# Another written order for the up-projection's prologue and units in a one-core hybrid decoder layer

## The chip, the cores and the metric

One core of a Trainium2 chip. The core has TensorE (PE, matrix products into PSUM banks), VectorE (DVE), ScalarE (ACT) and GpSimd (POOL), and SyncE (SP), which here only issues transfers. Each engine runs its own instructions in the order in which the program gives them, and waits on semaphores for the others. Transfers are issued from SP's, ACT's and POOL's queues. The metric is the device time of one execution in microseconds; given are the median, the lowest and the highest of three runs.

## The reference, cut to what matters

The kernel computes one decoder layer on 512 tokens of 1024 channels: a modulated norm, an input projection, two groups of attention-like heads, an output projection, then a gated MLP. The change is in the first half of the MLP:

```python
h2 = rmsnorm(x, norm2_g[l]) * (1.0 + sc2) + sh2
u = causal_dwconv(h2 @ w_up[l], conv_w[l], conv_b[l])      # w_up: 1024 x 5632
a, v = jnp.split(u, 2, axis=-1)
x = x + gt2 * ((jax.nn.silu(a) * v) @ w_down[l])           # w_down: 2816 x 1024
```

All arrays are f32, and the products are made to f32 accuracy.

## The kernel before

**Products.** Every f32 operand is split into a high and a low part (hi is the operand rounded to the PE's f32 form by a cast on ACT, L149; lo is the operand minus hi, a subtraction on DVE, L150), and a product is three matmuls: hi x hi, hi x lo, lo x hi (`mm3`, L152 to L155). The up-projection goes column by column: 22 pairs of a gate column block and a value column block, each 128 wide, so 44 *steps* numbered st. A step multiplies 8 blocks of weights with all 512 tokens: 24 matmuls of 128x512, into one PSUM bank `u`. After a step comes `up_post(st)`: bias and last tap of the convolution on ACT (L1621), the two other taps on DVE (L1622, L1623), silu on ACT (L1626) for a gate step, and for a value step the gate product (L1629) and then a list of small *work items* that split the result for the down-projection (L1801 and L150 on DVE, L149 on ACT; two parts are parked in memory by ACT's queue, L1831 and L1832).

**Units.** Steps 8 to 23 are done in four *units* j = 2 to 5 of four steps. In a unit the first two steps (4j, 4j+1) are not made as 48 full matmuls but, in the manner of Strassen and Winograd, as seven products of half size (P1 to P7, each 12 matmuls of 128x256) on sums and differences of weights and of tokens. The other two steps (4j+2 and 4j+3, called B and C) are standard and are cut into B0, B1 and C0, C1. Between the half products small moves are needed: S copies the bank of P1 (ACT, L1755) before P6 adds more into it; w copies the bank of P5 aside (ACT, L1711); V and W add that copy back (DVE, L1759 and L1761).

**Weights.** Each 1 MB load `up_i` comes in two pieces of 512 KB from SP's queue into one of three raw buffers; a load is issued two loads ahead, and waits until the last reader of its buffer is done. The forms of the seven half products are made by n1, ns, nc, na, s4, n5 (split, sums and differences) and f2, f3, f4, f6, f7 (casts and subtractions of half size). The standard weights B and C are made in two ways. *Split*: cast on ACT, subtraction on DVE. *Added*: ACT writes the negated weights (L1682, in the prologue L256), a transfer on POOL's queue adds the raw weights in place and rounds (L1683, L257), and ACT casts hi (L1684, L258); this uses no DVE. In a unit m0' and m1' start B's and C's added form for the next unit, and h0' and h1 cast their hi parts. The buffers of these forms are few (two for hi and lo, one more shared with n1 and n5), so a form waits for the step that last used the buffer.

**The written order.** The scheduler is switched off. The program emits instructions in the order of two strings of tokens: PRO for the prologue (steps 1 to 7 and the preparation of unit 2) and UNIT, which is run for j = 2, 3, 4, 5. A token emits its instructions on the engines that it needs, so one string sets the queues of PE, ACT, DVE, POOL and SP at once. M1 to M7 are standard steps, Fk and Ak make the weights of step k in the split or the added form, qk (in a unit p-1, p0, p1, p2, for step 4j-1 to 4j+2) is `up_post`, t is one of eight token sums and their splits, x is one work item. A token with ' belongs to the next unit. CUT gives how many of the eight weight blocks are in B0 and C0.

Lines that the prediction speaks of: S is L1755, w L1711, V and W L1759 and L1761, m0' and m1' L1682 and L1683, h0' and h1 L1684, all token kinds are in `do_`. Line numbers are those of the kernel before; the kernel after has one line more from the table on, so its rows read one higher.

Of the kernel before, what the change touches and what calls it, by code (L numbers as in the profile page):

```python
# [39 lines left out]
LAG = 4  # L40
NB = 2
NU = 5
CUT = {"B": 6, "C": 6}
PRO = ("x t t M1 t t F3 F4 t t M2 A5 q0 q1 t M3 A6 t M4 q2 x q3 M5 F7 q4 x x x M6 q5 n1' f2' ns' M7 nc' n5' q6 na' s4' x m0' f4' x f7' x m1' x x x x f6'")
UNIT = ("P1 P5 f3 S n1' w ns' B0 P6 P2 V B1 x x P7 p-1 n5' f2' h1 x P3 W x f4' C0 m0' p2 P4 x nc' na' s4' x x h0' C1 p0 p1 x x m1' f6' x x f7' x")
PREP = ('sq2 sq3 rq2 rq3', '', 'nq0', 'fq0', 'nq1', '', 'lq0', 'fq1', 'nq2', '', 'lq1', 'fq2', 'nq3', 'lq2', 'fq3',
        'lq3', 'sk0 rk0 sk1 rk1', 'nk0 fk0 sk2 rk2', 'nk1 fk1 sk3 rk3', 'lk0 nk2 fk2', 'lk1 nk3 fk3 sa0 ra0',
        'sa1 ra1 lk2 na0 fa0', 'sa2 ra2 lk3 na1 fa1', 'sa3 ra3 la0 na2 fa2', '', 'la1 na3 fa3', '', 'la2', '', 'la3',
# [60 lines left out]
def hybrid_layer_kernel(ctx: ExitStack, tc: tile.TileContext, d: dict, out: bass.AP, dbg=None):  # L109
    nc = tc.nc  # L110
# [13 lines left out]
    def nm(s):  # L124
        uid[0] += 1
        return f"{s}_{uid[0]}"
# [7 lines left out]
    def TMP(shape, dt=F32, tag="tmp"):  # L134
        n = 1
        for a in shape[1:]:
            n *= a
        if n > 256:
            return tp.tile(shape, dt, tag="t2", name=nm(tag), bufs=9)
        return tp.tile(shape, dt, tag="t1", name=nm(tag), bufs=4)  # L140
# [4 lines left out]
    def f32(ap):  # L145
        return ap.bitcast(F32)

    def split(hi, lo, src, eng=None):
        sc.copy(hi, src)  # L149
        (eng or ve).tensor_tensor(lo, src, f32(hi), ALU.subtract)  # L150
# [74 lines left out]
    def take(name):  # L225

        i = taken[0]
        assert loads[i][0] == name, (loads[i][0], name)
        while len(issued) < min(i + (5 if loads[min(len(issued), len(loads) - 1)][0][0:2] in ("dx", "dy") else 3), len(loads)):
            issue()  # L230
        taken[0] += 1
        return issued[i]
# [1369 lines left out]
    wts = {}  # L1602

    def up_mm(st, sl, ks=range(KT)):
        if st not in us:
            us[st] = PS("u")
            if st not in wts:
                wts[st] = next_parts(st < nst - 2)
        hi, lo = wts[st]
        for k in ks:  # L1610
            mm3(us[st][:, sl], hi[:, k], lo[:, k], h2T[k // 2][0][:, k % 2, sl], h2T[k // 2][1][:, k % 2, sl],
                k == 0 and not sl.start, k == KT - 1)
# [23 lines left out]
    raws = {}  # L1636
# [41 lines left out]
    def std_form(src, added):  # L1678
        hi = wp.tile(list(src.shape), F32R, tag="whi", name=nm("whi"))
        lo = wp.tile(list(src.shape), F32R, tag="wlo", name=nm("wlo"))  # L1680
        if added:
            sc.activation(lo, src, AF.Copy, scale=-1.0)  # L1682
            gp.dma_start(f32(lo), src, accum_op=ALU.add)  # L1683
            return (hi, lo), lambda: sc.copy(hi, src)  # L1684
        split(hi, lo, src)
        return (hi, lo), None
# [11 lines left out]
    high = {}  # L1698

    def std_make(j, s):  # L1700
        st = 4 * j + 2 + s
        if s == 0:
            raws[j] = take(f"up{2 * j + 1}")
        wts[st], high[st] = std_form(raws[j][:, s], s or j > NB)

    def seed(o, src):
        sc.copy(o, src)
# [15 lines left out]
    def do(j, tok):  # L1723
        last = j == NU
        if tok.endswith("'"):
            if last:
                if tok in ("n1'", "m0'"):
                    piece()
                return
            return do_(j + 1, tok[:-1])  # L1730
        return do_(j, tok)

    def do_(j, tok):
# [18 lines left out]
        elif tok in ("B0", "B1", "C0", "C1"):  # L1752
            up_mm(4 * j + (2 if tok[0] == "B" else 3), full, (range(0, CUT[tok[0]]), range(CUT[tok[0]], KT))[int(tok[1])])
        elif tok == "S":
# [3 lines left out]
        elif tok == "V":  # L1758
            ve.tensor_tensor(u(0, hi_), u(1, lo_), ws5[j], ALU.add)  # L1759
        elif tok == "W":  # L1760
            ve.tensor_tensor(u(1, hi_), u(1, lo_), ws5[j], ALU.add)  # L1761
        elif tok[0] == "p":
            up_post(4 * j + int(tok[1:]))
        elif tok == "x":
            step(1)
        elif tok == "t":
            turn()
        elif tok[0] == "m":
            std_make(j, int(tok[1]))
        elif tok[0] == "h":  # L1770
            h = high.pop(4 * j + 2 + int(tok[1]))
            if h:
                h()
        elif tok == "n1":
            pair_open(j)
        elif tok == "ns":
            pair_sum(j)
        elif tok == "nc":
            pair_less(j, 2, 0, 2)
        elif tok == "na":  # L1780
            pair_less(j, 0, 4, 0)
        elif tok == "s4":
            pair_less(j, 1, 1, 0)
        elif tok == "n5":
            split(*w[5], quads[j][4])
        else:
            pair_form(j, int(tok[1]), {6: 0, 2: 1, 7: 2, 3: 1, 4: 3}[int(tok[1])])
# [5 lines left out]
    h1, h2 = slice(0, 256), slice(256, 512)  # L1793
# [156 lines left out]
    made[0] = 1  # L1950
    for tok in PRO.split():
        if tok[0] == "M":
# [13 lines left out]
    for j in range(NB, NU + 1):  # L1966
        for tok in UNIT.split():
            do(j, tok)
# [80 lines left out]
    for q in range(NQ):  # L2049
        w = ready.pop(0)  # L2050
# [7 lines left out]
    for a in range(2):  # L2058
        t = TMP([P, T])
        ve.tensor_tensor(t, bR[a], gt2[:, lead], ALU.mult)  # L2060
        ve.tensor_tensor(rest[2 + a][:, lead], rest[2 + a][:, lead], t, ALU.add)
    for bank, a, cols in ((bS[0], 0, lead), (bS[1], 1, slice(0, 256)), (bV[0], 1, slice(256, 512))):
        for n, (hi, lo, j) in enumerate(ws):
            mm3(bank[:, cols], *stat(4, j, a), hi[:, cols], lo[:, cols], n == 0, n == len(ws) - 1)
        t = rest[2 + a][:, cols]
# [23 lines left out]
```

## Time and profile before

| | |
|---|---|
| median of three runs | 683.36 us |
| lowest, highest | 682.51, 684.45 us |
| the profiled execution | 684.09 us |
| its span on the core | 682.3 us |
| granted PE clock in the span | 1.0 |
| PE busy | 671.6 us (98%) |
| DVE, ACT, POOL busy | 574.1, 377.7, 53.8 us |

In the profile the up-projection runs from 330.8 us to 573.7 us. The prologue's order begins near 343 us. P1 of unit 2, 3, 4 and 5 starts at 376.33, 398.59, 420.97 and 442.65 us, and the first step behind the units at 464.02 us. Rows of a timeline read: start, duration, engine, line, operation, out<-in by the program's names, shape, and in brackets how long the engine was idle before and what ended it. Names carry no buffer numbers there. Ends of matmuls are modelled, so the distance from one matmul's start to the next one's says more than a busy time.

### The profile page before, as it was taken

What the parts mean: (1) busy time and instruction counts of PE and PEld (TensorE: products, weight loads), DVE (VectorE), ACT (ScalarE), POOL (GpSimd) and SP (SyncE); (2) the same over time, 40 slices, a digit from 0 to 9 for tenths busy, and PEclk for the clock granted to TensorE, in tenths of its full rate; (3) what the DMA queues carried; (4) which work ended last, traced back from release to release, by engine and by line L of the source; (5) the groups of instructions that cost most, each with busy time, mean ns of one, the idle gap of its engine ahead of it and who ended that gap; (6) DMA issues with size and microseconds to landing.
All of it is one profiled execution on the core that took longest, in us unless ns stands there. A gap on an engine that the chain in (4) does not pass through costs nothing.

```text
span 682.3 us, 10584 instructions
## 1 busy us (share of the span) xinstructions
PE 671.6 (98%) x3892; PEld 562.6 (82%) x3893; DVE 574.1 (84%) x1129; ACT 377.7 (55%) x729; POOL 53.8 (8%) x72
## 2 busy tenths in 40 slices
PE   8999999999999999999999999999999999999997
PEld 4677798788988888888998889888888888888886
DVE  4588988998899898687878988988888888988787
ACT  5564346665577678435665666664454455553441
POOL 1006243200000000200000010000000000000000
PEclk9999999999999999999999999999999999999999
DMA  9997643496123132535345567976754643959932
GB/s 279 271 322 232 205 159 124 125 293 201 32 93 125 32 93 97 183 105 149 124 98 149 136 146 182 232 186 200 205 166 138 215 161 125 375 210 400 394 110 93
DMA packets 108745, 122.23 MB, mean 179 GB/s; under 512 B 6875, under 2 KB 84499, under 8 KB 108693
## 3 DMA queue, kind: packets, MB, share of 16 engines
q1 hardware_dynamic: 103253, 105.84, 49.6%
q10 hardware_dynamic: 4144, 10.99, 4.7%
q0 software_dynamic: 1296, 4.72, 3.6%
q8 instruction: 31, 0.51, 0.3%
q14 instruction: 21, 0.17, 0.1%
HBM read 103.96 MB, written 12.85 MB: 171 GB/s over the span
## 4 chain that ended last, share of the span: by engine, by line
PE 71%; DVE 12%; DMA 6%; SPq 4%; ACT 4%; issue 2%; ACTq 0%; POOL 0%; DVEq 0%; POOLq 0%
PE u L153 7%; PE u L154 7%; PE u L155 7%; PE dn L154 5%; PE dn L155 5%; PE dn L153 5%; DMA raw<-in_w_up 3%; PE pT L153 3%; PE pT L155 3%; PE pT L154 3%; PE oT L1082 3%; PE F L1054 3%; SPq L314 3%; PE oh L155 2%; PE oh L153 2%; PE oh L154 2%
## 5 line engine op out<-in xcount | busy, mean ns | idle before, releaser
L155 PE MATMUL u<-h2h,wlo 128*128 128x512 f32 (+1 forms) x224 | 83.8, 374 | 0.5 <-DVE wlo L150 0.5
L153 PE MATMUL u<-h2h,whi 128*128 128x512 f32 (+1 forms) x224 | 84.2, 376 | 0.0
L154 PE MATMUL u<-h2l,whi 128*128 128x512 f32 (+1 forms) x224 | 83.9, 375 | 0.0
L150 DVE TENSOR_TENSOR wlo<-raw,whi 128x1024 fp32r<-128x1024 f32 (+1 forms) x47 | 56.5, 1203 | 12.2 <-ACT whi L149 12.0
L149 ACT CAST whi<-raw 128x1024 fp32r<-128x1024 f32 (+1 forms) x47 | 47.7, 1015 | 33.2 <-PE u L154 16.1
L155 PEld LDWEIGHTS u<-h2h,wlo 128*128 128x128 f32 x224 | 42.2, 188 | 8.5 <-DVE wlo L150 1.0
L153 PEld LDWEIGHTS u<-h2h,whi 128*128 128x128 f32 x224 | 42.2, 189 | 7.3 <-ACT whi L149 0.2
L154 PEld LDWEIGHTS u<-h2l,whi 128*128 128x128 f32 x224 | 42.3, 189 | 6.8
L1022 ACT ACTIVATE pt<-pt,mx 128x128 f32<-128x128 f32 (+3 forms) x64 | 35.9, 562 | 16.4 <-DVE mx L1006 16.1
L1622 DVE SCALAR_TENSOR_TENSOR y<-u,cv,y 128x511 f32<-128x511 f32 x44 | 32.8, 745 | 12.7 <-ACT y L1621 12.7
L1626 ACT ACTIVATE y<-y 128x512 f32<-128x512 f32 x21 | 13.3, 633 | 49.2 <-DVE y L1623 49.2
L153 PE MATMUL pT<-hT,whi 128*128 128x512 f32 x96 | 38.7, 404 | 0.0
L155 PE MATMUL pT<-hT,wlo 128*128 128x512 f32 x96 | 37.6, 392 | 0.0
L154 PE MATMUL pT<-hT,whi 128*128 128x512 f32 x96 | 37.6, 391 | 0.0
L155 PE MATMUL u<-h2h,w 128*128 128x512 f32 (+1 forms) x104 | 37.1, 357 | 0.0
L154 PE MATMUL u<-h2l,w 128*128 128x512 f32 (+1 forms) x104 | 37.1, 356 | 0.0
L153 PE MATMUL u<-h2h,w 128*128 128x512 f32 (+1 forms) x104 | 37.1, 356 | 0.0
L1623 DVE SCALAR_TENSOR_TENSOR y<-u,cv,y 128x510 f32<-128x510 f32 x44 | 32.9, 749 | 1.5
L1621 ACT ACTIVATE y<-u,cv 128x512 f32<-128x512 f32 x44 | 34.0, 772 | 0.0
L1006 DVE CUSTOM_DVE_ANT_0 pt<-S,cmask 128x128 f32<-128x128 f32 (+3 forms) x64 | 29.7, 485 | 4.5 <-PE S L1001 4.5
L1061 ACT COPY pT<-F 128x512 f32<-128x512 f32 (+2 forms) x52 | 25.8, 498 | 13.9 <-PE F L1054 13.5
L390 POOL TENSOR_TENSOR hrs<-hrs,mhalf 128x4 f32<-128x4 f32 (+2 forms) x16 | 20.2, 1267 | 136.7 <-DVE hrs L389 136.6
(453 smaller groups left out, 1938.8 us busy)
## 6 DMA issues: line engine op xcount, KB each, us to landing
raw<-in_w_up SPq DMA_DIRECT2D x44, 512.0 KB
ada<-in_w_ada SPq DMA_DIRECT2D x48, 256.0 KB
aw<-in_w_ada SPq DMA_DIRECT2D x24, 512.0 KB
raw<-in_w_down SPq DMA_DIRECT2D x10, 1024.0 KB
raw<-in_w_in SPq DMA_DIRECT2D x7, 1024.0 KB
rawd<-in_w_down SPq DMA_DIRECT2D x12, 512.0 KB
pk<-st ACTq DMA_DIRECT2D x11, 512.0 KB
S<-pk SPq DMA_DIRECT2D x11, 512.0 KB
```

Of the source, the lines that this page charges most:

```text
L149: sc.copy(hi, src)
L150: (eng or ve).tensor_tensor(lo, src, f32(hi), ALU.subtract)
L153: pe.matmul(o, ah, bh, start=start, stop=False, skip_group_check=True)
L154: pe.matmul(o, ah, bl, start=False, stop=False, skip_group_check=True)
L155: pe.matmul(o, al, bh, start=False, stop=stop, skip_group_check=True)
L314: sp.dma_start(t[:, :, e], ada_first[:, 4 * half:4 * half + 4, e, k * P:(k + 1) * P])
L1006: ve.tensor_tensor_reduce(pt[:, sl], ps[:, sl], cmask[:, 512 - W:512], -1.0, 1e30, ALU.add, ALU.min, mx[:, e:e + 1])
L1022: sc.activation(pt[:, sl], pt[:, sl], AF.Exp, bias=mx[:, e:e + 1], scale=-1.0, accum_out=su[:, h % 2, e:e + 1])
L1061: sc.copy(pT, ps[:, 0:n * P])
L1621: sc.activation(y, u, AF.Identity, bias=cv[:, 132 + c:133 + c], scale=cv[:, 88 + c:89 + c])
L1622: ve.scalar_tensor_tensor(y[:, 1:], u[:, :T - 1], cv[:, 44 + c:45 + c], y[:, 1:], ALU.mult, ALU.add)
L1623: ve.scalar_tensor_tensor(y[:, 2:], u[:, :T - 2], cv[:, c:c + 1], y[:, 2:], ALU.mult, ALU.add)
```

## The change

The two strings and one entry of CUT are others, and a constant ADD is added that keeps the condition as it was: with (1, 1) the expression `ADD[s] and (s or j > NB)` has the truth of `(s or j > NB)`.

```diff
-CUT = {"B": 6, "C": 6}
-PRO = ("x t t M1 t t F3 F4 t t M2 A5 q0 q1 t M3 A6 t M4 q2 x q3 M5 F7 q4 x x x M6 q5 n1' f2' ns' M7 nc' n5' q6 na' s4' x m0' f4' x f7' x m1' x x x x f6'")
-UNIT = ("P1 P5 f3 S n1' w ns' B0 P6 P2 V B1 x x P7 p-1 n5' f2' h1 x P3 W x f4' C0 m0' p2 P4 x nc' na' s4' x x h0' C1 p0 p1 x x m1' f6' x x f7' x")
+CUT = {"B": 6, "C": 5}
+ADD = (1, 1)
+PRO = ("t x t M1 t t t M2 t F3 M3 F4 t A5 q0 q1 F6 q2 M4 q3 M5 M6 x t A7 q4 x x x q5 n1' ns' nc' f2' n5' q6 M7 na' s4' x m0' x f4' m1' x f7' f6' x x x x")
+UNIT = ("P1 S P5 w n1' B0 x ns' x f3 P6 f4' P2 V p-1 n5' B1 h1 P7 W p2 P3 C0 nc' m0' x x na' P4 x f7' x h0' f2' p0 s4' C1 x p1 m1' x f6' x x x x")
...
-        wts[st], high[st] = std_form(raws[j][:, s], s or j > NB)
+        wts[st], high[st] = std_form(raws[j][:, s], ADD[s] and (s or j > NB))
```

The instructions are the same but for two weights of the prologue: step 6 takes the split form in place of the added one, step 7 the added in place of the split. SP's queue has the same rows. On PE the order P1 P5 B0 P6 P2 B1 P7 P3 C0 P4 C1 stays, and one weight block of C goes from C0 to C1.

ACT in the middle of unit 2, before, from p-1's bias (`y_4418`) to the silu of p0. `wlo_4473` is m0', `y_4476` p2 and its silu, `whi_4299` h1, `whi_4472` h0', `y_4507` p0:

```order
L1621 ACTIVATE y_4418<-u_4246,cv 128x512
L149 CAST w_826_4345<-e_4350 128x512
L149 CAST wq_4428<-raw_4235 128x512
L1684 CAST whi_4299<-raw_4115 128x1024
L149 CAST wq_4447<-raw_4235 128x512
L1682 ACTIVATE wlo_4473<-raw_4282 128x1024
L1621 ACTIVATE y_4476<-u_4352,cv 128x512
L1626 ACTIVATE y_4476<-y_4476 128x512
L149 CAST gQ_4423<-y_4274 128x256
L1684 CAST whi_4472<-raw_4282 128x1024
L1621 ACTIVATE y_4507<-u_3874,cv 128x512
L1626 ACTIVATE y_4507<-y_4507 128x512
```

The same place of the change (`y_4403` is p-1, `wlo_4471` m0', `y_4433` p2, `whi_4470` h0', `y_4498` p0):

```order
L1622 ACTIVATE y_4403<-u_4254,cv 128x512
L150 CAST w_826_4344<-e_4368 128x512
L1685 CAST whi_4294<-raw_4115 128x1024
L1622 ACTIVATE y_4433<-u_4347,cv 128x512
L1627 ACTIVATE y_4433<-y_4433 128x512
L1683 ACTIVATE wlo_4471<-raw_4282 128x1024
L150 CAST wq_4490<-raw_4235 128x512
L1685 CAST whi_4470<-raw_4282 128x1024
L150 CAST wq_4495<-raw_4235 128x512
L1622 ACTIVATE y_4498<-u_3874,cv 128x512
L1627 ACTIVATE y_4498<-y_4498 128x512
```

p2 and its silu stand ahead of m0' now; f7' (`wq_4490`) and f2' (`wq_4495`) stand around h0'.

ACT from p1 of unit 2 to S and w of unit 3, before (`y_4512` is p1, `wlo_4524` m1', `wq_4527` f6', `wq_4534` f7', `wq_4563` f3 of unit 3, `u_3874` is written by S, `w_853` by n1', `w5u_4573` by w; the rest are work items):

```order
L1621 ACTIVATE y_4512<-u_4312,cv 128x512
L149 CAST st_832_4424<-y_4274 128x256
L149 CAST gP_4233<-s_807_4234 128x256
L1682 ACTIVATE wlo_4524<-raw_4282 128x1024
L149 CAST wq_4527<-raw_4235 128x512
L149 CAST gQ_4423<-s_807_4234 128x256
L149 CAST st_833_4425<-s_807_4234 128x512
L149 CAST wq_4534<-raw_4235 128x512
L149 CAST wq_4563<-raw_4235 128x512
L1755 COPY u_3874<-u_4537 128x256
L149 CAST w_853_4570<-raw_4342 128x512
L1711 COPY w5u_4573<-ux_4538 128x256
```

The same place of the change, from the last work items on (`st_834` is the last split of the pair, `wq_4597` is f3 of unit 3, `gP_4520` a work item):

```order
L150 CAST st_834_4410<-s_807_4234 128x512
L1756 COPY u_3874<-u_4537 128x256
L1712 COPY w5u_4564<-ux_4538 128x256
L150 CAST w_853_4569<-raw_4341 128x512
L1832 DMA pk_3611<-st_833_4409 128x512
L1833 DMA pk_3610<-st_834_4410 128x1024
L150 CAST gP_4520<-y_4498 128x256
L150 CAST wq_4597<-raw_4235 128x512
```

S stands right behind the work items, f3 behind w, n1', the two parking transfers and a work item.

ACT in the prologue, before (`w_791` are A6's two instructions, `hS_4122` is the fourth t, `whi_4191` F7, `y_4195` q4):

```order
L256 ACTIVATE w_791_4118<-raw_3837 128x1024
L258 CAST w_791_4118<-raw_3837 128x1024
L149 CAST hS_4122<-hB_3712 128x1024
L1621 ACTIVATE y_4151<-u_3950,cv 128x512
L1626 ACTIVATE y_4151<-y_4151 128x512
L149 CAST gP_4084<-y_4074 128x256
L1621 ACTIVATE y_4158<-u_4090,cv 128x512
L149 CAST whi_4191<-raw_3837 128x1024
L1621 ACTIVATE y_4195<-u_4126,cv 128x512
```

and in the change (`w_791` is F6, `wlo_4216` and `whi_4215` are A7, `y_4220` is q4):

```order
L150 CAST w_791_4118<-raw_3837 128x1024
L1622 ACTIVATE y_4121<-u_3950,cv 128x512
L1627 ACTIVATE y_4121<-y_4121 128x512
L1622 ACTIVATE y_4151<-u_4062,cv 128x512
L150 CAST gP_4113<-y_4103 128x256
L150 CAST hS_4211<-hB_3712 128x1024
L257 ACTIVATE wlo_4216<-raw_3837 128x1024
L259 CAST whi_4215<-raw_3837 128x1024
L1622 ACTIVATE y_4220<-u_4126,cv 128x512
```

F6 has its subtraction on DVE now, and F7's subtraction ahead of q4 is gone.

## The prediction

> **What bounds the kernel now.** I read the page's busy shares first, then the waits of PE from 330 to 590 us, then PE's timeline around each wait, then the chain of waits, and last the ACT, DVE and POOL timelines of one unit. One row of the page and one of PE's waits:
>
> ```profile
> PE 671.6 (98%) x3892; PEld 562.6 (82%) x3893; DVE 574.1 (84%) x1129; ACT 377.7 (55%) x729; POOL 53.8 (8%) x72
> ...
> PE u L153 <- ACT u L1755: 1.5, 2, 1.1
> ```
>
> PE sets the end, and an order can only win the time in which PE starts nothing. Matmul ends are modelled, so I take the distance from start to start:
>
> ```profile
> 378.96 0.28 PE L154 MATMUL ux<-hS,w 128*128 128x256 f32 x1
> 379.08 0.28 PE L155 MATMUL ux<-hS,w 128*128 128x256 f32 x1
> 379.39 0.50 PE L153 MATMUL u<-h2h,whi 128*128 128x512 f32 x1
> ...
> 380.65 0.50 PE L155 MATMUL u<-h2h,wlo 128*128 128x512 f32 x1 [0.53 <-DVE wlo L150]
> 380.99 0.39 PE L153 MATMUL u<-h2h,whi 128*128 128x512 f32 x1
> ...
> 405.12 0.39 PE L154 MATMUL u<-h2l,whi 128*128 128x512 f32 x1
> 405.35 0.39 PE L155 MATMUL u<-h2h,wlo 128*128 128x512 f32 x1
> 406.82 0.39 PE L153 MATMUL u<-hS,wq 128*128 128x256 f32 x1 [1.09 <-ACT u L1755]
> 407.05 0.28 PE L154 MATMUL u<-hS,wq 128*128 128x256 f32 x1
> ...
> 427.73 0.39 PE L155 MATMUL u<-h2h,wlo 128*128 128x512 f32 x1
> 428.50 0.39 PE L153 MATMUL u<-hS,wq 128*128 128x256 f32 x1 [0.38 <-ACT u L1755]
> 428.72 0.28 PE L154 MATMUL u<-hS,wq 128*128 128x256 f32 x1
> ...
> 449.40 0.39 PE L155 MATMUL u<-h2h,wlo 128*128 128x512 f32 x1
> 449.85 0.39 PE L153 MATMUL u<-hS,wq 128*128 128x256 f32 x1
> 450.08 0.28 PE L154 MATMUL u<-hS,wq 128*128 128x256 f32 x1
> ```
>
> Undisturbed, a half-width matmul takes 0.12 us (378.96 to 379.08) and a full one 0.227 (405.12 to 405.35). At B0 of unit 2 the four steps from 379.08 to 380.99 took 1.91 instead of 0.12 + 3 x 0.227 = 0.80: **1.11 lost**. At P6 the two steps from the last matmul of B0 should take 0.347; they took 1.70, 0.99 and 0.68 in units 3, 4 and 5: **1.35, 0.64 and 0.33 lost**. Together 3.43 us; nothing else between 330 and 590 us stands still for over 0.15. So 3.43 is also the most that the change can win.
>
> Why P6 waits: it adds into a bank that S (ACT, L1755) must copy first. S stands behind a loop that the chain of waits shows:
>
> ```profile
> 385.03 8.24 DMA raw<-in_w_up
> ...
> 407.59 0.69 DVE wq L150
> 408.30 6.65 DMA raw<-in_w_up
> ...
> 415.05 1.06 ACT wlo L1682
> ...
> 429.97 6.32 DMA raw<-in_w_up
> ```
>
> f3's subtraction on DVE (ended 408.27) frees a weight buffer; SP loads up_{2j+5} into it; m0' (ACT L1682, at 393.38 and 415.05) needs that load; everything queued behind m0' on ACT follows, S and the next f3 among it. From m0' to m0' this took 21.67 us. PE's work of a unit is 84 x 0.12 + 48 x 0.227 = 20.98, some 21.03 with the slower first steps after each change of width. The loop is longer than the work, so it paces PE.
>
> **The change, part by part.** No instruction is added or removed, SP's queue is the same, and PE's differs only by three matmuls of C (0.68 us) that move behind P4. What counts is the ACT and DVE queues.
>
> *Units: m0' behind p2.* ACT's rows of one unit before:
>
> ```profile
> 393.38 1.06 ACT L1682 ACTIVATE wlo<-raw 128x1024 fp32r<-128x1024 f32 x1 [4.47 <-DMA raw<-in_w_up]
> 394.34 0.76 ACT L1621 ACTIVATE y<-u,cv 128x512 f32<-128x512 f32 x1
> 396.76 0.63 ACT L1626 ACTIVATE y<-y 128x512 f32<-128x512 f32 x1 [1.66 <-DVE y L1623]
> ...
> 397.60 1.04 ACT L1684 CAST whi<-raw 128x1024 fp32r<-128x1024 f32 x1
> 398.54 0.77 ACT L1621 ACTIVATE y<-u,cv 128x512 f32<-128x512 f32 x1
> 401.26 0.63 ACT L1626 ACTIVATE y<-y 128x512 f32<-128x512 f32 x1 [1.95 <-DVE y L1623]
> 401.80 0.76 ACT L1621 ACTIVATE y<-u,cv 128x512 f32<-128x512 f32 x1
> ...
> 404.03 0.60 ACT L149 CAST wq<-raw 128x512 fp32r<-128x512 f32 x1
> 404.54 0.40 ACT L149 CAST gQ<-s 128x256 fp32r<-128x256 f32 x1
> ...
> 406.41 0.36 ACT L1755 COPY u<-u 128x256 f32<-128x256 f32 x1
> ```
>
> ACT stood 4.47 us for the load, and p2 (394.34, silu 396.76) came only then. From m0' to p1 (401.80) took 8.42. In the new queue p2 and its silu run ahead of m0', inside that idle time. Behind m0' (0.96 to the next start, as at 393.38) come f7' (0.51, as at 404.03), h0' (0.94, as at 397.60) and f2' (0.51), so p0 starts at m0' + 2.93. Its two DVE products and the hand-overs put its silu 2.41 later (before 2.72, with one more subtraction ahead of them), then 0.53 and a 0.30 cast: p1 at m0' + 6.17, **2.25 earlier**. From p1 to the end of f3 on DVE it took 6.47 (401.80 to 408.27). f3 now stands behind w, n1', ns' and two work items; in start distances: 0.82 to p1's first product, 0.80 + 0.80 + 0.65 for its products and the gate, 0.34 + 0.60 + 0.33 + 0.33 + 0.60 for parts and f6', 0.60 + 0.60 for n1' and ns', 0.33 for a part, 0.69 for f3: about 7.45, **0.98 later**. So the loop loses 1.27: 13.62 + 0.09 + the load. With the loads of the rows above that is 20.0 (6.32), 20.4 (6.65) or 22.0 (8.24) against 21.03 of PE work: below PE's work with two of them, above it with one.
>
> *S and P6.* S moves up too: f3 and f7' (0.52 each) leave the stretch between p1 and S. Laid out from unit 2's load at its 8.24: f3 ends at 385.5, m0' starts at 393.9, p1 at 400.05, then m1' 0.96, two 512-casts, four 256-casts and f's hand-overs, and S ends by 404.0. P1 of unit 3 starts at 397.2, and P1, P5 and B0 take 24 x 0.12 + 18 x 0.227 = 6.97, so P6 is not due before 404.2. S is ready, by 0.2 in unit 3 and by 1.5 and more in units 4 and 5, whose loads were shorter. The 1.35 + 0.64 + 0.33 are won.
>
> *What is late next: B0's weights.* m0' starts an accumulating transfer on POOL's queue that completes B0's low part for the next unit:
>
> ```profile
> 394.79 0.89 POOL L1683 DMA_DIRECT2D wlo<-raw  x1 [11.69 <-ACT wlo L1682]
> ...
> DMA to landing us min/median/max: 5.1/5.8/6.0
> ...
> w<-raw POOLq DMA_DIRECT2D x1, 512.0 KB, 7.3
> ```
>
> It starts 0.35 after m0' ends, so in unit 2 at 395.2, and lands at 400.3 to 401.2. B0 of unit 3 starts at 400.1 and needs the low part in its third matmul, 0.45 later: 400.56. That is a **new stall of 0 to 0.7** with the 8.24 load, and none if the load takes 6.65 (everything 1.6 earlier). Units 4 and 5 have 0.6 and more to spare. I take 0.35, the middle. On this the Trainium skill (DMA: Bandwidth & Descriptors, Queues, rings and completion order) has a rule: each DMA engine goes round its queues packet by packet, so transfers of different queues that overlap stretch each other. By it unit 2's load would shorten, since its neighbour, the accumulate of m1', now starts 2 us earlier against it, and the new stall would be 0: 3.43 instead of 3.08. The profile names no cause for the 8.24, so I keep the row.
>
> *Prologue.* B0 of unit 2 lost 1.11 because its split weights were late:
>
> ```profile
> 366.61 1.22 DVE L150 TENSOR_TENSOR wlo<-raw,whi 128x1024 fp32r<-128x1024 f32 x1
> 367.75 0.74 DVE L1622 SCALAR_TENSOR_TENSOR y<-u,cv,y 128x511 f32<-128x511 f32 x1
> ...
> 378.30 1.04 ACT L149 CAST whi<-raw 128x1024 fp32r<-128x1024 f32 x1
> 379.37 1.23 DVE L150 TENSOR_TENSOR wlo<-raw,whi 128x1024 fp32r<-128x1024 f32 x1
> ```
>
> F7's subtraction (1.22, at 366.61) sat ahead of q4's products. F7 becomes A7 (an accumulate, no DVE work), and A6 becomes F6, which subtracts near 358.3, where no matmul waits for DVE. Laid out, q4's products start at 366.2, q5, n5' and q6 follow 1.5 to 1.8 earlier, m0' casts at 377.0 and its low part is done at 379.3. B0 starts at 379.15 and needs it at 379.6: **1.11 won, 0.3 to spare**. A7 has a price of its own: its transfer starts at 364.9 and lands at 370.0 to 370.9; M7 starts at 370.8 and needs it at 371.3. Covered by 0.4; at the 7.3 of the other form it is 0.9 late. The load behind it (up6) starts at 370.9 instead of 367.86 and is wanted at 382.7: free. F3's low part ends at 348.8, M3 is due at 349.07: free. CUT costs nothing: P4 comes 0.68 earlier, and its f4' and W are done 4 us ahead.
>
> Sum: -3.43 + 0.35 = -3.1 on the profiled execution's 684.09 (span 682.3): 681.0. It ran 0.7 above the median of 683.36, so **680.3** as a median.
>
> **The rivals.** *Half of it.* The accumulates take the 7.3 of one prologue row in their new places. M7 then waits 0.9 and B0 of unit 3 about 1.1 more, unit 4 another 0.2: 3.43 - 2.2 = 1.2 won, 682.1. For: A7 is a prologue transfer as that one was. Against: seven of eight landed within 6.0.
>
> *Given back.* The down-projection is bound by its loads, and starts 3 us earlier only to wait:
>
> ```profile
> 573.70:682.30 108.60, 105.18 (x472) 87.08 (x470) 92.61 (x107) 45.70 (x55) 0.00 (x0) 1.00 0.69 254
> ```
>
> Here PE is idle 3.4 us in all, nearly all of it the way of the last outputs, and the DMA share is 0.69; its loads wait for buffers that PE frees, and so move with PE. It would give 683.4.
>
> *Slower.* The loop through the load becomes longer. h1 now follows f3 by 1.9 us instead of 3.4, so the next pair of load pieces is issued into the first. If this made the first piece 2 us longer in each unit (10.2, 8.7, 8.3), m0' in unit 2 would come 2 later, B0 of unit 3 would stand 2.6, and each of the next two units 1.0 (loop of 22.1 against 21.03): 4.6 lost against 3.43 won, 684.5. It decides from about 1.6 us more per load. Against: both loads stand in one SP queue, and with the same distance the rows show 6.32, 6.65 and 8.24.
>
> **How the numbers follow.** Forecast 0.78, half 0.11, given back 0.06, slower 0.05. Own range of the forecast: 0 to 0.7 of new stall gives 679.9 to 680.6, and 0.8 either way for the spread of the runs shown. Down to 679.2; up to 682.2, which takes in half of it. About 0.3% (2.05 us) is what can be told from no change: faster 0.80, same 0.15, slower 0.05.
>
> **What would show it.** Right: PE's waits on ACT u L1755 gone, P1 to P1 near 21.0 in all four units, ACT's longest idle before m0' with p2 already done, m0' to m0' at PE's pace. The prologue step: m0's cast near 377 and no wait for DVE at B0. Wrong: a wait of PE for an accumulated wlo (M7, or B0 of unit 3), loads of over 8 us in more than one unit, or PE idle after 590 us.

## The result, and the profile after

The changed kernel takes 679.68 us in the median of six runs (678.73 to 680.09), the kernel before on the same chip 683.1 (682.2 to 684.45): a ratio of 0.9946, 95% interval 0.9933 to 0.9959, so 2.8 to 4.6 us less. The forecast was 680.3 in a range of 679.2 to 682.2.

The page's engine row, of the changed kernel:

```profile
PE 668.8 (99%) x3892; PEld 562.9 (83%) x3893; DVE 574.3 (85%) x1129; ACT 378.0 (56%) x729; POOL 53.9 (8%) x72
```

The list of PE's waits from 330 to 590 us is empty: no wait for S, none for the split weights. PE's timeline at the two kinds of place where it stood before, B0 of unit 2 and P6 of unit 3 (start, duration, engine, line, operation):

```profile
377.61 0.28 PE L156 MATMUL ux<-hS,w 128*128 128x256 f32 x1
377.73 0.40 PE L154 MATMUL u<-h2h,whi 128*128 128x512 f32 x1
377.96 0.40 PE L155 MATMUL u<-h2l,whi 128*128 128x512 f32 x1
378.20 0.39 PE L156 MATMUL u<-h2h,wlo 128*128 128x512 f32 x1
...
402.65 0.39 PE L156 MATMUL u<-h2h,wlo 128*128 128x512 f32 x1
402.88 0.28 PE L154 MATMUL u<-hS,wq 128*128 128x256 f32 x1
402.99 0.28 PE L155 MATMUL u<-hS,wq 128*128 128x256 f32 x1
```

Starts are 0.23 apart at full width and 0.12 at half width, and the steps from one to the other are no longer. (Lines have moved by one: the added constant.) The windows of one unit's length (the window, its length, the busy times of PE, PEld, DVE, ACT and POOL, then the granted clock, the DMA share and GB/s) say the same:

```profile
376.30:397.30 21.00, 21.00 (x134) 19.04 (x133) 19.51 (x35) 15.68 (x29) 1.75 (x2) 1.00 0.73 189
397.30:418.30 21.00, 21.00 (x134) 19.04 (x133) 18.45 (x33) 14.16 (x26) 1.73 (x2) 1.00 0.76 188
418.30:439.30 21.00, 21.00 (x134) 19.04 (x134) 18.41 (x33) 14.16 (x26) 1.75 (x2) 1.00 0.74 188
```

The two profiled spans differ by 5.0 us (682.3 and 677.3), more than the medians do. Part of that is not the change's. The same product of the out projection, far ahead of anything that it touches, in the kernel before and then in the changed one:

```profile
312.10 0.39 PE L154 MATMUL oh<-wol,mixN 128*128 128x512 f32 x1
```

```profile
310.66 0.39 PE L155 MATMUL oh<-wol,mixN 128*128 128x512 f32 x1
```

The profiled run of before was 1.44 late by then. In the other profiled runs below this part ends anywhere from 0.3 earlier to 1.0 later than in the changed kernel. So I compare from a fixed matmul to the last one: from PE's matmul number 1800 (271.89 before, 270.45 after) to the last it took 406.71 us before and 403.18 after, **3.53 less**. That is all of the 3.43 that PE had lost.

### The profile page after: what moved, and what is told of

Same layout as the page of the kernel before. It is cut to its first block, busy times and chain, and to the rows that moved or that the text cites. A ratio compares the mean times of both kernels' runs of the same rounds, so it can differ in the third digit from the quotient of the medians.

```text
span 677.3 us, 10574 instructions
## 1 busy us (share of the span) xinstructions
PE 668.8 (99%) x3892; PEld 562.9 (83%) x3893; DVE 574.3 (85%) x1129; ACT 378.0 (56%) x729; POOL 53.9 (8%) x72
## 4 chain that ended last, share of the span: by engine, by line
PE 90%; DVE 5%; DMA 3%; ACT 1%; issue 1%; SPq 0%; POOL 0%; ACTq 0%; DVEq 0%; POOLq 0%
PE u L154 11%; PE u L155 11%; PE u L156 11%; PE dn L155 5%; PE dn L156 5%; PE dn L154 5%; PE pT L154 3%; PE pT L156 3%; PE pT L155 3%; PE oT L1083 3%; PE F L1055 3%; PE oh L156 2%; PE oh L154 2%; PE oh L155 2%; DMA ada<-in_w_ada 2%; PE lev L1183 2%
```

## The experiments

For each kernel the table gives what PE lost at the six places: for every step of over 0.245 us from start to start, what lies above 0.227. (The prediction's 1.11, 1.35, 0.64 and 0.33 also count the slower step just behind a stall.) "To the end" is the stretch from that fixed matmul to the last, "median" that of the runs. M6 and B0 of unit 2 belong to the prologue.

| kernel | M6 | B0, unit 2 | P6, unit 2 | P6, unit 3 | P6, unit 4 | P6, unit 5 | to the end | median |
|---|---|---|---|---|---|---|---|---|
| before | 0 | 1.00 | 0.02 | 1.25 | 0.54 | 0.23 | 406.7 | 683.1 |
| changed | 0 | 0 | 0 | 0 | 0 | 0 | 403.2 | 679.7 |
| e1, new UNIT alone | 0.34 | 0.76 | 0 | 0 | 0 | 0 | 404.3 | 680.5 |
| e2, new PRO alone | 0 | 0 | 0 | 0 | 0.50 | 0.32 | 404.2 | 681.1 |
| e3, m0' behind p2 alone | 0.24 | 0.87 | 0.02 | 0.09 | 0.10 | 0.10 | 405.0 | 681.4 |
| e4, S ahead alone | 0.37 | 0.74 | 0 | 0.52 | 0.27 | 0.31 | 405.7 | 682.0 |
| e5, changed, m0' ahead of p2 | 0 | 0 | 0 | 0 | 0 | 0 | 403.2 | 679.9 |
| e6, 6 and 7 exchanged alone | 0 | 0.94 | 0.03 | 0.85 | 0.35 | 0.22 | 406.1 | 683.4 |
| e9, changed, 6 and 7 put back | 1.07 | 0 | 0 | 0 | 0 | 0 | 404.3 | 680.5 |
| e10, F3 and F4 later alone | 1.26 | 0 | 0 | 1.30 | 1.04 | 0.46 | 407.7 | 683.7 |
| e11, both prologue edits | 0 | 0 | 0 | 0.66 | 1.06 | 0.50 | 405.8 | 682.2 |
| e12, f3 behind ns' alone | 0.22 | 0.88 | 0 | 0.40 | 0.22 | 0.13 | 405.4 | 682.3 |
| e13, m1' without its transfer | 0.16 | 0.91 | 0.68 | 0 | 0 | 0 | 405.3 | 681.8 |
| e14, changed, f3 back in front | 0 | 0 | 0 | 0 | 0 | 0 | 403.1 | 679.9 |

The median of before lay between 683.06 and 683.45 beside the different kernels; each ratio below is to the before that ran beside it.

Where the old PRO stands with A6 (e1, e3, e4, e12, e13), M6 loses 0.16 to 0.37, waiting for A6's transfer, and B0 then loses that much less: the two add up to 1.07 to 1.11 in each. Counted from the fixed matmul, the low part that B0 waits for is done at the same time in all five and in before, 108.7 us. It is one delay, met at two places. The prediction, from a profiled run with nothing lost at M6, could not see this.

### The two halves: e1 and e2

e1 is the kernel before with the new UNIT and `"C": 5`; e2 is the kernel before with the new PRO.

```diff
e1:
-CUT = {"B": 6, "C": 6}
+CUT = {"B": 6, "C": 5}
-UNIT = (the old order)
+UNIT = (the new order)
e2:
-PRO = (the old order)
+PRO = (the new order)
```

> The kernel before with the new UNIT and its CUT alone; PRO and its F6-less form stay as before. Loop theory (the unit's length was set by f3, then the load, m0', p2, p1 and S; m0' behind p2 shortens it): PE no longer waits at P6 of units 3, 4 and 5 (1.35 + 0.64 + 0.33 = 2.32 won), and the stall of 1.11 at B0 of unit 2 stays, since only PRO was to take it away; profile about 681.8 if the accumulating transfers take the 4.5 to 5.1 of the changed kernel, 682.1 if they take the 5.8 of before. Backlog theory (the three shrinking stalls are what the prologue left behind, and decay by themselves): the prologue is as late as before, so P6 still loses 1 or more in unit 3; profile 683 or more.

> The kernel before with the new PRO alone; UNIT and CUT stay as before. Loop theory: B0 of unit 2 waits for nothing (1.11 won), and P6 of units 3, 4 and 5 still waits for S, 1.4 + 0.7 + 0.4, as long as the loads take the 8.2, 6.7 and 6.3 of before; profile about 683.0. Backlog theory: no waits at P6 either, profile about 680.6. Load theory (the changed prologue shortens the loads and the accumulating transfers by more than 1 us, because they overlap less): also no waits at P6, but then the load of unit 2 lands in less than 6.7 us instead of 8.24.

e1 has a ratio of 0.9959 to before (0.9944 to 0.9974). No time is lost at P6 in any unit though the prologue is as late as ever, so the backlog theory is out. e2 (0.9968, 0.9952 to 0.9984) loses nothing in B0, and at P6 0.50 and 0.32 in units 4 and 5, so the waits do not go away with the prologue. But in unit 3 it loses nothing where before lost 1.25, which the loop theory had not foreseen. Its chain of waits says why, with the load of unit 2 (start, us, what):

```profile
383.39 6.78 DMA raw<-in_w_up
```

It took 6.78 us, against 8.24 before. The load had become 1.46 shorter although nothing in it changed; counted from the fixed matmul it was also issued 1.15 earlier, so it landed 2.6 earlier, while PE, without the stall at B0, was 1.0 earlier. The load theory had asked for under 6.7 and no wait at any P6: the load came near, the waits of units 4 and 5 stayed.

The two gains, 2.4 and 2.5 to the end, add up to 4.9 and not 3.53. The wait at P6 of unit 3 can be removed by either, and is counted in both.

### Which move of UNIT: e3, e4 and e5

```diff
e3, in the kernel before:
-C0 m0' p2 P4
+C0 p2 m0' P4
e4, in the kernel before:
-P1 P5 f3 S n1' w ns'
+P1 S P5 f3 n1' w ns'
e5, in the changed kernel:
-W p2 P3 C0 nc' m0' x x
+W P3 C0 nc' m0' p2 x x
```

> The kernel before with one exchange in UNIT: m0' behind p2, nothing else. Loop theory: this alone moves p1 and S up by about 2.7 us behind the load and so takes the waits at P6 away (2.32 won); the stall at B0 of unit 2 stays at 1.11. What m0' loses, 0.96 of ACT, makes the low part for the next B0 late by 0 to 0.7 in unit 3 if its transfer takes 5.8, by nothing if it takes 4.6; profile 681.8 to 682.4. Queue theory (S late because f3 stands ahead of it on ACT and DVE, not because of m0'): P6 still loses over 1 us in unit 3; profile 683.3 or more.

> The kernel before with one exchange in UNIT: S directly behind P1, ahead of P5 and f3, as the changed kernel has it; m0' stays ahead of p2. Loop theory: S is late because p1 is late, and p1 because m0' waits for the load; f3 takes only 0.3 of ACT and 0.5 of DVE out of S's way and starts as much later itself, so P6 of unit 3 still loses 1.0 or more, units 4 and 5 still 0.3 to 0.8; about 0.3 won in all, 683.1 by the median. Queue theory (f3 ahead of S is what makes it late): no loss at P6 of units 4 and 5, under 0.8 in unit 3; 681.5.

> The changed kernel with one token put back: m0' ahead of p2 again (and ahead of the two work items' successors), all else as changed. Loop theory: the loop through f3, the load, m0', p2, p1 and S is then longer than before the change, because f3 now stands behind w and n1' as well; PE waits at P6 of every unit, 1.3 + 0.6 + 0.3 if the loads take 1.5 less than before, 2.8 + 2.1 + 1.8 if they take as long; 682 to 686. Shorter-transfers theory (the changed order keeps loads and accumulating transfers apart, and that took the waits away, wherever m0' stands): no wait over 0.3 at P6 in any unit; 680.

e3 (0.9974, 0.9963 to 0.9984) shows that the exchange of m0' and p2 is enough by itself: 0.1 is left at each P6. The 0.1 returns in every unit because the loop is still a little longer than PE's work: S ended at 383.06, 404.28, 425.53 and 446.77, 21.2 apart. e4 (0.9987, 0.9977 to 0.9996) lies between the two theories: S ahead of f3 takes 0.9 of the 2.0 at P6, more than the 0.3 of the loop theory; but 0.27 and 0.31 stay in units 4 and 5, where the queue theory had none.

e5 went against the loop theory as I had put it (0.9959, 0.9944 to 0.9974): m0' stands ahead of p2 again and PE waits nowhere. Its list of PE's waits is as empty as the changed kernel's; ACT's waits from 380 to 450 us show that m0' does wait for the load again:

```profile
389.39 1.06 ACT L1683 ACTIVATE wlo<-raw 128x1024 fp32r<-128x1024 f32 x1 [2.83 <-DMA raw<-in_w_up]
399.23 1.04 ACT L1683 ACTIVATE wlo<-raw 128x1024 fp32r<-128x1024 f32 x1
410.99 1.06 ACT L1683 ACTIVATE wlo<-raw 128x1024 fp32r<-128x1024 f32 x1 [3.17 <-PE u L156]
...
ACT wlo L1683 <- DMA raw<-in_w_up: 5.9, 2, 3.1
```

(The middle row is m1'.) From m0' to m0' it is 21.60, still longer than PE's unit. What differs is the reserve. Between the end of S and the start of P6 lie 0.70, 1.13, 0.56 and 0.09 us in units 2 to 5 of e5: the loop eats half a microsecond per unit, and the units are over when the reserve is. In the changed kernel these are 0.70, 2.23, 2.24 and 2.24. The loop theory was right on the slope and wrong on the start: I had not seen how much the other moves put in hand. Most of that is the load. Issued at 385.00 it was in by 389.39, 4.4 us or less instead of 8.24. That the rest of the reserve is due to the other moves is argued, not tested one by one.

### Why the load is shorter: e12, e13 and e14

The new theory: a load that runs beside other transfers is stretched by them, above all by the accumulating transfer of m1', which in the old order is still under way when f3 starts the load.

```diff
e12, in the kernel before:
-P1 P5 f3 S n1' w ns' B0 P6
+P1 P5 S n1' w ns' f3 B0 P6
e13, in the kernel before:
-        wts[st], high[st] = std_form(raws[j][:, s], s or j > NB)
+        wts[st], high[st] = std_form(raws[j][:, s], not s and j > NB)
e14, in the changed kernel:
-P1 S P5 w n1' B0 x ns' x f3 P6
+P1 S P5 f3 w n1' B0 x ns' x P6
```

> The kernel before with one token moved in UNIT: f3 behind w, n1' and ns', so that the load that it starts is issued about 2 later, when the accumulating transfer of m1' has landed; m0' stays ahead of p2. The prediction's costing (the load takes the 8.2, 6.7 and 6.3 of its rows wherever it starts): m0' comes 2 later, and P6 loses 2.3, 1.9 and 1.6; 686. Overlap theory (a load that starts under the accumulating transfer is stretched by about what it overlaps, and takes 4.7 to 5.3 if it starts behind it): the load takes under 5.6 in units 3 and 4 and lands within 0.5 of where it landed before, counted from P1; P6 loses no more than in the kernel with only S ahead (0.5 + 0.25 + 0.3); 681.5 to 682.5.

> The kernel before with m1' formed by a cast and a subtraction on DVE (1.23 more on DVE in each unit) in place of the accumulating transfer; the order of the steps is as before. The output is the same. Overlap theory (that transfer is what stretches the load which m0' waits for): the load takes 4.7 to 5.3 in units 3 and 4, against 6.65 and 6.32, and under 7.5 in unit 2, where two other transfers of ACT's queue still run; the waits at P6 go. If the load takes over 6.2 in units 3 and 4, the accumulating transfer is not what stretches it. Prologue stall at B0 stays, about 1; 680.5 to 682.5, unless the added DVE work opens a wait of its own.

> The changed kernel with f3 put back behind P5, ahead of w, n1' and ns', so that its load is issued about 2 earlier. Overlap theory: the load overlaps the end of m1's transfer again by up to 1 and takes 5.2 to 6.5 instead of 4.7 to 4.9 in units 3 and 4, landing at most 1 earlier than in the changed kernel. Without such an effect it takes 4.7 to 4.9 and lands 2 earlier. By both no wait of PE (p2 stands ahead of m0'): 679.3 to 680.0.

The load that m0' waits for, from issue to its last record of completion in the trace; how long the transfer of m1' was still under way when it was issued; and what two other queues moved between the load's issue and its landing, POOL's (the transfer of m1') and ACT's (the parking stores). Units 2, 3 and 4:

| kernel | load, us | beside m1's transfer, us | moved by POOL's queue, MB | by ACT's queue, MB |
|---|---|---|---|---|
| before | 8.24, 6.65, 6.32 | 2.4, 1.3, 1.5 | 0.32, 0.09, 0.07 | 0.52, 0.66, 0.69 |
| e12, f3 later | 6.44, 5.14, 5.05 | 0.9, 0.5, 0.4 | 0.05, 0, 0 | 0.52, 0.42, 0.40 |
| e13, no such transfer | 3.99, 4.16, 4.10 | none | 0 | 0.15, 0.02, 0.02 |
| changed | 5.04, 4.74, 4.89 | none | 0 | 0.13, 0.25, 0.23 |
| e14, changed, f3 earlier | 7.34, 5.54, 6.84 | 1.4, 0.7, 0.7 | 0.14, 0.01, 0.01 | 0.52, 0.79, 0.79 |

The rows behind the last two columns for unit 3 of before, the changed kernel and e14, in this order (queue, kind: packets, MB, share of 16 engines; q10 is ACT's queue, q0 POOL's):

```profile
q10 hardware_dynamic: 228, 0.66, 37.8%
q0 software_dynamic: 38, 0.09, 7.0%
...
q10 hardware_dynamic: 76, 0.25, 13.8%
...
q10 hardware_dynamic: 288, 0.79, 49.9%
q0 software_dynamic: 19, 0.01, 1.6%
```

In the chain of waits of e12 the load's two rows stand as follows (start, us, what); before they were 8.24 and 6.65:

```profile
385.60 6.44 DMA raw<-in_w_up
...
408.27 5.14 DMA raw<-in_w_up
```

e12 (0.9986, 0.9976 to 0.9996) is the plainest. Its run was 0.77 ahead of that of before at the fixed matmul; counted from there, the load of unit 2 was issued 1.3 later (385.60 against 385.03) and landed 0.5 earlier (392.04 against 393.27). The prediction's costing, in which the load keeps its length, would have lost 5.8 at P6; it lost 0.75. e13 (0.9979, 0.9969 to 0.9988) takes the transfer away and the load takes 4.0 to 4.2 in all three units, less than the 4.7 to 5.3 expected, and P6 of units 3 to 5 waits no more; DVE's added subtraction shows as a wait of 0.68 within P6 of unit 2. In e13 the second store on ACT's queue is also issued only behind the load (406.34 against 404.80 in unit 3), and ACT's queue moves 0.02 MB in the load's time in units 3 and 4, so its 4.1 is the load nearly clear of both, and e13 does not tell the two apart. e14 (0.9951, 0.9935 to 0.9967) is the counterproof: counted from the fixed matmul, the load of unit 3 was issued 1.5 earlier than in the changed kernel and landed 0.7 earlier, and those of units 2 and 4, issued 1.8 and 1.5 earlier, landed 0.5 and 0.4 later. Here two stores of ACT's queue overlap it too (400.36 to 404.27 and 402.24 to 406.65 in unit 3).

So other transfers do stretch the load, but "above all" is not borne out. In unit 2 the transfer of m1' counts: before, e12 and e14 have the same 0.52 MB of stores in the load's time, and the load takes 8.24 with 0.32 MB of that transfer, 7.34 with 0.14 and 6.44 with 0.05. In units 3 and 4 it moves at most 0.09 MB, and the load goes with the stores: 4.1 to 4.2 us at 0.02 MB, 4.7 to 4.9 at about a quarter of a MB, 5.1 at 0.4, 6.3 to 6.7 at 0.7, 5.5 and 6.8 at 0.79. The changed order avoids both, because f3 now stands behind the two parking stores as well. This is read from the packets; no run moves the stores alone.

This is what the rule of the Trainium skill says (DMA: Bandwidth & Descriptors, Queues, rings and completion order: each engine takes turns between its queues, packet by packet). The trace agrees as far as the lengths go: 8.24 down to 5.04, with the traffic of the other two queues down from 0.84 MB to 0.13.

The accumulating transfers answer in the same way. POOL's rows of m0' and m1' in the changed kernel, and the landing times of the group from 370 to 470 us (min, median, max):

```profile
391.92 0.89 POOL L1684 DMA_DIRECT2D wlo<-raw  x1 [12.36 <-ACT wlo L1683]
398.78 0.87 POOL L1684 DMA_DIRECT2D wlo<-raw  x1 [5.97 <-ACT st L150]
412.95 0.86 POOL L1684 DMA_DIRECT2D wlo<-raw  x1 [13.30 <-ACT wlo L1683]
...
DMA to landing us min/median/max: 4.5/4.5/5.1
```

Before it was 5.1, 5.8 and 6.0. In e13 the loads come out first and it is m0's transfer that overlaps them: 6.8, 7.1 and 7.2.

### The prologue: e6, e9, e10 and e11

```diff
e6, in the kernel before:
-M3 A6 t M4 q2 x q3 M5 F7 q4
+M3 F6 t M4 q2 x q3 M5 A7 q4
e9, in the changed kernel:
-q1 F6 q2 M4 q3 M5 M6 x t A7 q4
+q1 A6 q2 M4 q3 M5 M6 x t F7 q4
e10, in the kernel before:
-M1 t t F3 F4 t t M2 A5 q0 q1 t M3 A6
+M1 t t t t M2 F3 F4 t A5 q0 q1 M3 A6
```

e11 is e10 with F and A of 6 and 7 exchanged as in e6.

> The kernel before with F and A of groups 6 and 7 exchanged in PRO (F6 where A6 was, A7 where F7 was), nothing else. The prediction's prologue step (F7's subtraction of 1.22 on DVE ahead of q4 was what made m0's low part late): the stall of 1.11 at B0 of unit 2 goes, or at least 1 us of it; profile about 683.0. Rival (the order of the small tokens behind q4, from n1' to m0', sets it; the 1.22 is taken up by waits of ACT and DVE on PE's q6): 0.8 or more of the stall stays; profile 683.8. The waits at P6 of units 3 to 5 stay by both.

> The changed kernel with F and A of groups 6 and 7 put back (A6, F7), all else as changed. The prediction's prologue step (F7's subtraction of 1.22 ahead of q4 makes m0's low part late): B0 of unit 2 waits again, 0.8 to 1.1; 680.7. Rival after the exchange in the kernel before did not take the stall away (F3 and F4, which wait for their load at the head of ACT's and DVE's queues with the sums and forms of h2 behind them, push one such form into the full stretch behind q1; the changed order has them done ahead): no wait over 0.3 at B0, 679.7 as the changed kernel.

> The kernel before with one edit in the head of PRO: F3 and F4 behind the next two turns of h2 and M2, and the following turn ahead of A5 instead of M3; A6, F7 and everything from q2 on stay as before. Rival of the prologue step (DVE stood idle 2.1 behind F3's subtraction, which waited for the load, and a form of h2 of 1.2 then fell into the full stretch ahead of m0'): the stall of 1.11 at B0 of unit 2 is gone, 0.2 at most stays. The prediction's step (F7's subtraction): 0.8 or more stays, because F7 is where it was. P6 of units 4 and 5 still waits 0.4 to 0.8 by both; unit 3 by 1.4 if its load takes 8.2, by nothing if it takes 6.9 as with the whole new PRO. 681.0 to 682.5.

> The kernel before with both prologue edits tried apart: F3 and F4 behind the next turns and M2, a turn ahead of A5, and F and A of groups 6 and 7 exchanged; UNIT as before. Two-part theory (the order of F3 and F4 takes away the wait at B0 of unit 2; the exchange of 6 and 7 takes away the wait at M6 for A6's transfer, which lands at 366 whenever it starts because up5's load runs beside it): no wait over 0.2 at M6 and at B0, as with the whole new PRO; P6 of units 3 to 5 loses 0 to 1.4, 0.7 and 0.5. 681.0 to 682.0. If something else of the new PRO is needed, 0.8 or more stays at B0 or M6: 682 to 683.

e6 is not told from before (0.9993, 0.9981 to 1.0004), and 0.94 stays at B0. Its third matmul of B0 waits for DVE as before:

```profile
378.84 0.50 PE L155 MATMUL u<-h2h,wlo 128*128 128x512 f32 x1 [0.53 <-DVE wlo L150]
```

So F7's subtraction ahead of q4 was not the whole cause, and the exchange by itself only traded it: A7 puts two ACT operations (L256 and L258, 0.95 apart) ahead of q4's first step, which started at 365.13. In the changed kernel it started at 364.06, counted from the fixed matmul 1.3 earlier.

e10 moves F3 and F4 behind the next turns of h2, leaves F7 where it was, and B0 waits no more. But PE has by then lost 1.26 at M6, which alone would cover B0's wait. What tells is when the low part for B0 is done, counted from the fixed matmul: before 108.7, e6 108.6, e10 108.8, e11 107.6, changed 107.4. Its rows of e10 and e11:

```profile
378.44 1.23 DVE L150 TENSOR_TENSOR wlo<-raw,whi 128x1024 fp32r<-128x1024 f32 x1
...
377.75 1.23 DVE L150 TENSOR_TENSOR wlo<-raw,whi 128x1024 fp32r<-128x1024 f32 x1
```

So neither edit alone brings it forward; both together do, by 1.2. What the move of F3 and F4 adds shows in DVE's and ACT's rows of the kernel before near 346 us:

```profile
344.15 1.22 DVE L150 TENSOR_TENSOR hS<-hB,hS 128x1024 fp32r<-128x1024 f32 x1
347.46 1.23 DVE L150 TENSOR_TENSOR w<-raw,w 128x1024 fp32r<-128x1024 f32 x1 [2.10 <-ACT w L149]
...
346.38 1.05 ACT L149 CAST w<-raw 128x1024 fp32r<-128x1024 f32 x1 [3.58 <-PE u L155]
```

ACT stood 3.58 us at F3's cast and DVE 2.10 at its subtraction, with h2's sums and forms queued behind. What it waited for is a weight buffer that PE had to read first, not the load that I named in the expectations. In e10 DVE works through this time:

```profile
344.23 1.22 DVE L1639 TENSOR_TENSOR hB<-hB,hB 128x1024 f32<-128x1024 f32 x1
345.37 1.22 DVE L150 TENSOR_TENSOR hS<-hB,hS 128x1024 fp32r<-128x1024 f32 x1
346.50 1.22 DVE L150 TENSOR_TENSOR w<-raw,w 128x1024 fp32r<-128x1024 f32 x1
```

One form less is then left for the full stretch from q1 to m0', 1.2 us on DVE, which is about the size of the stall and of what e11 has over e6.

e10 as a whole gains nothing (1.0007, 0.9997 to 1.0017), because the delay is met at M6 instead, and e9 has the same wait (0.9967, 0.9955 to 0.9978). M6 needs A6's accumulated low part. First e10's rows, then the row of before (out, queue, count, KB, us to landing):

```profile
365.96 0.50 PE L155 MATMUL u<-h2h,w 128*128 128x512 f32 x1 [0.99 <-DMA w<-raw]
...
356.39 0.87 POOL L257 DMA_DIRECT2D w<-raw  x1 [5.70 <-ACT w L256]
...
w<-raw POOLq DMA_DIRECT2D x1, 512.0 KB, 9.5
```

```profile
358.42 0.86 POOL L257 DMA_DIRECT2D w<-raw  x1 [6.67 <-ACT w L256]
...
w<-raw POOLq DMA_DIRECT2D x1, 512.0 KB, 7.3
```

Counted from the fixed matmul, e10's was issued 1.0 earlier than that of before and landed 1.25 later; e9's, issued at 356.86 and landed at 366.2, also 1.0 earlier and 1.1 later. That is what M6 loses, 1.26 and 1.07. Two pieces of a load are issued just ahead of it (355.96 and 356.37 in e10); in e9 these were in by 360.4 and 362.7, so they do not explain all of it. From its issue at 356.39 to 359.9 the trace of e10 has packets of the load's queue alone, 0.64 MB of them, so a part is a late start; why the transfer then lasts until 366 stays open. So the exchange of 6 and 7 has a purpose after all, another than I gave: F6 needs no transfer at that time, and A7's, in a quiet stretch, took 4.6. e11 has both edits and no wait at M6 or B0 (0.9983, 0.9973 to 0.9992): these two are enough for the prologue, and neither is by itself. Its P6 waits are the old unit's.

## Why the prediction was right

*PE bounds, 3.43 is the most to be won: right.* 3.53 less to the end, with no wait left.

*m0' behind p2: right in its sizes, and enough by itself, but not what the gain hangs on.* From m0' (390.51) to p1 (396.70) it took 6.19; the prediction had 6.17. From p1 to the next load's issue (404.15) 7.45, where it had about 7.45 to the end of f3 (its terms add up to 7.49). e3 shows that the exchange is enough alone. e5 shows that with the other moves in place it could have been left out in this program of four units.

*The load: mis-sized, the step that failed.* "I keep the row", 8.24, and with it m0' at 393.9 on the clock of before. The load took 5.04, and m0' started at 390.51, or 391.95 with the 1.44 of the early part: 1.95 earlier. It no longer waited for the load at all. ACT's rows:

```profile
389.98 0.63 ACT L1627 ACTIVATE y<-y 128x512 f32<-128x512 f32 x1 [2.90 <-DVE y L1624]
390.51 1.05 ACT L1683 ACTIVATE wlo<-raw 128x1024 fp32r<-128x1024 f32 x1
```

The 2.90 is p2's silu, waiting for its own products on DVE. So the sign "ACT's longest idle before m0' with p2 already done" did not show: the idle time is ahead of the silu. From m0' to m0' it is 21.04 (390.51 to 411.55), PE's pace, instead of a loop of 22.0 and then 20.4.

*S: ready, with 2.2 to spare in unit 3* where 0.2 was forecast, for the same reason.

*The new stall: 0, not 0.35.* Both of its terms were too long, the load and the accumulating transfer (4.88 instead of 5.1 to 6.0). The low part landed at 396.8, some 2.4 before B0 needed it. Its place in the sum is the whole difference between the forecast gain of 3.1 and the 3.43 that the rule of the Trainium skill gave; the rule was weighed and set aside because no row of the kernel before showed a cause for the 8.24. e12 and e14 now do, and so does the count of packets in that load's time in the kernel before, 0.32 MB from POOL's queue and 0.52 MB from ACT's; the prediction named the first neighbour only.

*Prologue: 1.11 won, as said, and laid out to the tenth.* m0's cast was forecast at 377.0 and its low part at 379.3. The rows of the changed kernel (to be read with the 1.44) have 375.57 and the end of this one:

```profile
376.64 1.23 DVE L151 TENSOR_TENSOR wlo<-raw,whi 128x1024 fp32r<-128x1024 f32 x1
```

That is 377.01 and 379.31. *The reason given was half of it.* The prediction named F7's subtraction and the exchange of 6 and 7; that F3 is "free" is all that it said of the other move, without which e6 still loses 0.94 at B0. The layout had all moves in it, and so came out right; the sentence named one of two edits that work only together, and as far as the 1.11 rests on that sentence, it was luck.

*The rivals.* Half of it: accumulating transfers of 7.3 in the new places would have cost 2.2; they took 4.6 (A7) and 4.9. It could have come true: e9 and e10 show a transfer of 9.3 and 9.5 a few microseconds earlier in the prologue. Given back in the down-projection: PE's last 491 matmuls took 109.67 us after and 109.63 before, so the gain stays. Slower through longer loads: the distance of the next pair of pieces did shrink (first to third issue 2.3 instead of 3.4 in unit 2), but the first piece became shorter, not longer.

## What to carry to other kernels

A transfer's length in a trace belongs to its neighbours as much as to its size: before an order that shifts transfers is costed with old rows, look at what else was under way in each row, and take the clear ones as the lower bound. When a stall disappears in a layout that contains many moves, undo the moves one at a time before naming the cause; here the named one alone did nothing, and another alone only met the same delay at an earlier step. A wait that is gone says little while another wait stands ahead of it: look at when the operand was ready. A stall at the end of a saturated stretch can come from idle time well ahead of it, here over 30 us, where an in-order queue stood behind one step that waited.

## What the runs showed of the hardware that was not expected

The same 512 KB load took 4.0 to 4.2 us where the other two queues moved 0.02 to 0.15 MB in its time (e13), 4.7 to 5.0 with 0.13 to 0.25 MB (units 2 to 4 of the changed kernel), and 6.3 to 8.2 with 0.75 to 0.84 MB (before). An accumulating transfer of 512 KB took 4.5 us clear of a load, 4.8 to 7.2 beside parts of a load, and 9.3 to 9.5 where two load pieces had been issued 0.02 to 0.6 ahead of it (7.3 where they were 1.4 to 1.8 ahead); there, issued 1.0 earlier, it landed 1.1 to 1.25 later. And the part of the program ahead of every edit, one and the same in all kernels here, ended anywhere within 1.7 us from run to run.
